# A conformer and sparse-attention trunk: one-column token sums and a GpSimd power in the norms, and a bias table skewed by 16 writes

## The chip, the cores and the metric

The kernel runs on one core of a Trainium2 chip. The metric is the device time of one execution in microseconds (us), as the median of three. The engines are TensorE (PE), VectorE (DVE), ScalarE (ACT) and GpSimd (POOL); SyncE (SP) here only issues DMA transfers. SBUF and PSUM are the two on-chip memories; PSUM has eight banks of 128x512 here.

## What is computed

Two layers of a decoder trunk on 512 tokens of width 1024 in float32. Layer 0 is a half-step SwiGLU feed-forward, a Conformer convolution module, a second feed-forward and a gated per-layer input embedding (ple); layer 1 has native sparse attention (nsa) in place of the convolution. Each part begins with an RMS norm, the convolution has a layer norm inside, and a last RMS norm ends the trunk. The parts that the change touches:

```python
def rms_norm(x, g):
    xf = x.astype(jnp.float32)
    y = xf * lax.rsqrt(jnp.mean(xf * xf, axis=-1, keepdims=True) + RMS_EPS)
    return (y * g.astype(jnp.float32)).astype(x.dtype)

def swiglu(x, wg, wu, wd):
    return (jax.nn.silu(x @ wg) * (x @ wu)) @ wd

def conformer_conv(h, w_pw1, b_pw1, w_dw, b_dw, ln_g, ln_b, w_pw2, b_pw2):
    u = h @ w_pw1 + b_pw1
    a, g = jnp.split(u, 2, axis=-1)
    u = a * jax.nn.sigmoid(g)
    u = lax.conv_general_dilated(...)  + b_dw      # depthwise, 31 taps, causal
    mu = jnp.mean(uf, axis=-1, keepdims=True)
    var = jnp.mean(jnp.square(uf - mu), axis=-1, keepdims=True)
    uf = (uf - mu) * lax.rsqrt(var + LN_EPS) * ln_g + ln_b
    return jax.nn.silu(uf) @ w_pw2 + b_pw2
```

Attention scores get a relative-position bias per head, rel_bias[bucket(t - s), head], for 16 heads.

## The kernel before

**Layout.** Activations lie transposed: tile k of x holds channels 128k to 128k+127 on the partitions and the 512 tokens along the free axis. So the sum over channels for a norm runs over partitions, and PE makes it by a product with a matrix of 1/1024.

**Weights.** They are streamed in units of 128x1024 (512 KB), in the order of their use. A float32 product is made of three passes, so each raw unit (`raw`, two buffers, loaded by SP at L201) is split: `wh` is the rounded copy (ACT, L219), `wl` the rest (L221, on POOL for the kinds in `CALM` from unit `CALM_FROM` on, else on DVE). Five buffers of each (`HLB`) run ahead of PE. L244 to L246 are the three passes, and a unit serves 24 matmuls. Inputs are split likewise: `prep` makes the high part on ACT (L292) and the low part on DVE (L293).

**Norms.** While a part adds its results to x, squares of the tiles are made and summed in `acc` (L309 to L313). `rfin` splits acc, `token_means` multiplies by the 1/1024 matrix (L344), which gives each token's mean on all partitions; `diagonal` reads out one value per token as a 128x4 tile (L336), `rsqrt` is a bit trick and three Newton steps on it (eleven DVE instructions, L322 to L327); `spread` transposes the result on PE back over all partitions (L353) and ACT copies it to R (L355). The first results of the next part are multiplied by R when they come out of PSUM. The order of PE puts the spreading some matmuls after the sums.

**Convolution.** The taps become block matrices for PE, made by POOL (L503). `tally` and `square` sum the filters' results and their squares about a mean `mid` taken from the first four tiles (`centre`). For the layer norm two products give the means (L693 and the line after it), `off` is the mean less mid (L697), `diagonal` reads both out, and eight times Y - off (POOL, L711), times R (DVE, L712), SiLU (ACT). PE works on `z_tiles`, p @ ple_w_in, as fill around it (`FILL`).

**The skewed table.** `bias_tables`, in the scheduler's order at the begin of ffn2 of layer 0, makes ext, a table of 16 heads x 640 distances on 16 partitions, and one DMA of the POOL queue writes it 128 times per head to DRAM, rows 641 apart (L745). In layer 1 `tt_load` reads it with rows 640 apart, so each key row comes shifted by one. `z_tiles` puts z into DRAM; it is read back in ple.

**The end.** `final` does the last norm in two halves of 256 tokens: sums, Newton, spreading (L1161), a copy Rf (L1163), and the scaling of eight tiles, five on DVE (L1172) and three on ACT and POOL (L1169, L1170).

**The order.** The code is issued once through; a scheduler of the language then decides each engine's order, and on an engine instructions run strictly in it. `high_priority(FIN_PRI)` moves instructions up.

Of the kernel before, what the change touches and what calls it, by code (L numbers as in the profile page):

```python
# [11 lines left out]
F32 = mybir.dt.float32  # L12
# [10 lines left out]
X_W1, SQ0, ADD0 = 4, 2, 4  # L23
# [4 lines left out]
CALM_FROM = 2  # L28
# [133 lines left out]
class Kern:  # L162
    def __init__(self, ctx, tc, aps):
# [31 lines left out]
    # -- weights --  # L195
    def _load(self, j):
        if KINDS[j] == "r":
            return
# [4 lines left out]

    def _split(self, j):
# [11 lines left out]
        if nsa and j % 4 in H_POOL:  # L216
            self.nc.gpsimd.tensor_copy(h[:, :w], t[:, :w])
        else:
            self.nc.scalar.activation(h[:, :w], t[:, :w], AF.Copy)  # L219
        eng = self.nc.gpsimd if calm or nsa and j % 4 in L_POOL else self.nc.vector  # L220
        eng.tensor_tensor(l[:, :w], t[:, :w], h[:, :w].bitcast(F32), op=OP.subtract)  # L221
        self.hl[j] = (h, l)

    def ahead(self, j):
        while self.next_split < min(j + 1, len(UNITS)):
            while self.next_raw < min(self.next_split + self.RAWB, len(UNITS)):
                self._load(self.next_raw)
# [3 lines left out]
        while self.next_raw < min(self.next_split + self.RAWB, len(UNITS)):  # L231
            self._load(self.next_raw)
# [15 lines left out]
    # -- small inputs --  # L248
# [25 lines left out]
    # -- norms: XH, XL = the two parts of x * g; R = 1 / rms along the free axis --  # L274
# [26 lines left out]
    def square_sum(self, k):  # L301
# [38 lines left out]
    def token_means(self, acc, eps):  # L340
# [946 lines left out]
```

## Time and profile before

| what | value |
|---|---|
| timed runs | 2169.51, 2168.81, 2167.43 us, median 2168.81 |
| profiled execution, span | 2167.5 us |
| PE busy | 2076.1 us (96%) |
| DVE busy | 1019.7 us (47%) |
| ACT busy | 830.8 us (38%) |
| POOL busy | 1051.4 us (49%) |
| DMA | 223.24 MB, mean 103 GB/s |

The page gives busy time by engine, groups of instructions by line, DMA issues with their landing, and the chain that ended last. The trace behind it gives timelines by engine, each with the idle time before an instruction and what ended it ("<-"). Durations of consecutive matmuls overlap, since they are pipelined; the distance between their starts is what one costs.

### The profile page before, as it was taken

How to read it: one execution, taken by the hardware profiler on the slowest of the kernel's cores; microseconds unless marked ns; L12 is line 12 of the kernel's file. 1: busy time of each engine (PE TensorE's matmuls, PEld its weight loads, DVE VectorE, ACT ScalarE, POOL GpSimd, SP SyncE). 2: the span in 40 equal slices, each digit the busy share in tenths (PEclk: the TensorE clock that was granted, in tenths of full speed). 3: DMA queues.
4: the chain of work that ended last, by engine and by line, in shares of the span. 5: the costliest groups of instructions: out<-in, count | busy, mean ns of one | idle time of the engine just before them, and what ended most of it. 6: DMA issues, size and time to landing. Idle time of an engine off the chain costs nothing. (4 is left out here: it accounts for less than half of the span.)

```text
span 2167.5 us, 25523 instructions
## 1 busy us (share of the span) xinstructions
PE 2076.1 (96%) x9546; PEld 1713.6 (79%) x9546; DVE 1019.7 (47%) x1889; ACT 830.8 (38%) x1393; POOL 1051.4 (49%) x653
## 2 busy tenths in 40 slices
PE   7999999899895999999999999999999999999997
PEld 6888888688674888888788888878888788888886
DVE  6430334797623312334743033355989673213336
ACT  4321234553522322234432123325888653223333
POOL 5444442784423444444444444556666444444441
PEclk9999999999997999999999999999999999999999
DMA  4222222244375222223322222454323032222222
GB/s 158 98 98 98 97 97 96 75 123 131 120 112 137 98 97 92 95 95 107 104 96 97 97 97 97 131 170 130 99 82 103 30 112 97 97 98 98 96 92 69
DMA packets 75882, 223.24 MB, mean 103 GB/s; under 512 B 8352, under 2 KB 16320, under 8 KB 75760
## 3 DMA queue, kind: packets, MB, share of 16 engines
q1 hardware_dynamic: 73728, 213.98, 29.6%
q0 software_dynamic: 1888, 7.59, 2.5%
q8 instruction: 75, 1.23, 0.2%
q14 instruction: 47, 0.39, 0.1%
q10 hardware_dynamic: 144, 0.07, 0.0%
HBM read 198.00 MB, written 16.25 MB: 99 GB/s over the span
## 5 line engine op out<-in xcount | busy, mean ns | idle before, releaser
L221 POOL TENSOR_TENSOR wl<-raw,wh 128x1024 fp32r<-128x1024 f32 (+1 forms) x315 | 787.6, 2502 | 900.6 <-ACT wh L219 871.5
L219 ACT ACTIVATE wh<-raw 128x1024 fp32r<-128x1024 f32 (+1 forms) x330 | 349.0, 1059 | 959.4 <-PE b L245 823.0
L244 PE MATMUL b<-s,wh 128*128 128x512 f32 x1728 | 678.8, 394 | 34.6 <-ACT R L355 22.8
L245 PE MATMUL b<-s,wh 128*128 128x512 f32 x1728 | 677.6, 392 | 6.1 <-DVE s L293 5.7
L246 PE MATMUL b<-s,wl 128*128 128x512 f32 x1728 | 677.2, 392 | 1.9 <-POOL wl L221 1.9
L244 PEld LDWEIGHTS b<-s,wh 128*128 128x128 f32 x1728 | 327.2, 189 | 103.7 <-ACT R L355 23.2
L245 PEld LDWEIGHTS b<-s,wh 128*128 128x128 f32 x1728 | 326.9, 189 | 77.2 <-DVE s L293 9.5
L246 PEld LDWEIGHTS b<-s,wl 128*128 128x128 f32 x1728 | 326.8, 189 | 71.2 <-POOL wl L221 2.8
L244 PE MATMUL b<-hid,wh 128*128 128x512 f32 x704 | 277.4, 394 | 0.0
L246 PE MATMUL b<-hid,wl 128*128 128x512 f32 x704 | 275.3, 392 | 0.0
L245 PE MATMUL b<-hid,wh 128*128 128x512 f32 x704 | 272.6, 388 | 0.0
L388 DVE TENSOR_TENSOR t<-b,R 128x512 f32<-128x512 f32 x88 | 60.8, 691 | 354.3 <-PE b L246 354.3
L426 DVE SCALAR_TENSOR_TENSOR s<-b,s 128x512 f32<-128x512 f32 x64 | 44.3, 692 | 331.2 <-PE b L246 331.2
L392 DVE TENSOR_TENSOR hid<-t,hid 128x512 fp32r<-128x512 f32 x88 | 170.2, 1937 | 53.4 <-ACT hid L391 53.2
L246 PEld LDWEIGHTS b<-hid,wl 128*128 128x128 f32 x704 | 132.2, 188 | 31.0
L245 PEld LDWEIGHTS b<-hid,wh 128*128 128x128 f32 x704 | 132.1, 188 | 29.6
L244 PEld LDWEIGHTS b<-hid,wh 128*128 128x128 f32 x704 | 132.3, 188 | 26.4
L386 DVE TENSOR_TENSOR t<-b,R 128x512 f32<-128x512 f32 x88 | 60.8, 691 | 166.5 <-PE b L246 96.0
L994 POOL TENSOR_SCALAR e<-e,sm,gates 128x512 f32<-128x512 f32 (+3 forms) x96 | 61.0, 640 | 41.2 <-DVE sm L988 35.6
L391 ACT ACTIVATE hid<-t 128x512 fp32r<-128x512 f32 x88 | 55.6, 633 | 55.9 <-DVE t L389 55.9
L389 DVE TENSOR_TENSOR t<-t,t 128x512 f32<-128x512 f32 x88 | 67.8, 774 | 8.0
L292 ACT ACTIVATE s<-s,small 128x512 fp32r<-128x512 f32 x48 | 38.0, 796 | 78.0 <-DVE s L426 34.9
(229 smaller groups left out, 2322.9 us busy)
## 6 DMA issues: line engine op xcount, KB each, us to landing
raw<-in_w SPq DMA_DIRECT2D x336, 512.0 KB, 3.5
skew<-tw POOLq DMA_DIRECT2D x1, 5120.0 KB, 56.4
z<-t SPq DMA_DIRECT2D x16, 256.0 KB, 2.4
z<-z SPq DMA_DIRECT2D x16, 256.0 KB, 3.3
tt<-skew SPq DMA_DIRECT2D x16, 256.0 KB, 2.8
wr<-in_w SPq DMA_DIRECT2D x8, 512.0 KB, 4.2
q<-t SPq DMA_DIRECT2D x32, 128.0 KB, 2.5
s<-in_xT SPq DMA_DIRECT2D x8, 256.0 KB, 6.1
```

The costliest lines, as they stand in the source:

```text
L219: self.nc.scalar.activation(h[:, :w], t[:, :w], AF.Copy)
L221: eng.tensor_tensor(l[:, :w], t[:, :w], h[:, :w].bitcast(F32), op=OP.subtract)
L244: mm(out, sh, mh, start=start, stop=False)
L245: mm(out, sh, ml, start=False, stop=False)
L246: mm(out, sl, mh, start=False, stop=stop)
L386: nc.vector.tensor_tensor(gr, pg, R, op=OP.mult)
L388: nc.vector.tensor_tensor(ur, pu, R, op=OP.mult)
L389: nc.vector.tensor_tensor(ur, ur, gr, op=OP.mult)
L391: nc.scalar.activation(h, ur, AF.Copy)
L392: nc.vector.tensor_tensor(l, ur, h.bitcast(F32), op=OP.subtract)
L426: nc.vector.scalar_tensor_tensor(self.xs[m], p, 0.5, self.xs[m], op0=OP.mult, op1=OP.add)
L994: nc.gpsimd.tensor_scalar(dst, dst, sm[:, a, bi:bi + 1], gate, op0=OP.mult, op1=OP.mult)
```

## The change

**Table.** ext goes to DRAM as `table`, 16x640. Each of 16 heads then has a DRAM tile of 128x641, written by one SP DMA that reads the head's table row 128 times (`skew_next`, called in `ffn` after each f above 2 while any is left). `tt_load` reads the tiles.

**Norms.** `rsqrt` is one POOL instruction, v to the power -0.5. `token_sums` makes one column per 128 tokens: the data tile is the stationary operand, one column of 1/1024 the moving one. `rfin(acc, True)`, for the two mix norms, takes the sums from acc at once, without the split and `diagonal`; the ffn and ple norms keep both. `spread_raw` leaves the result in PSUM.

**Layer norm.** off is made in its PSUM bank, the two sums come as columns (`mid0` is mid's column), the square of u is on ACT, Y - off moves from POOL to DVE, and Y times R reads R from PSUM.

**Final norm.** Its sums come as columns, and DVE's scalings read the spread values from PSUM.

**Start.** Unit 0 is loaded and split in halves, the order of the first loads is changed, 12 matmuls on constants run first, all squares are on ACT and all additions on DVE, and units 2 to 5 have their low parts on DVE (`CALM_FROM` 6).

```diff
-X_W1, SQ0, ADD0 = 4, 2, 4
+X_W1, WARM = 4, 12
...
-CALM_FROM = 2
+CALM_FROM = 6
...
+    def pieces(self, j, w):
+        return (slice(0, w // 2), slice(w // 2, w)) if j == 0 else (slice(0, w),)
...
+        self.power = self.cpool.tile([128, 4], F32, name="power")
+        nc.vector.memset(self.power, -0.5)
...
+        p = self.bank()
+        for n in range(WARM):
+            nc.tensor.matmul(p, self.meanr, self.meanr[:, None, :].to_broadcast([128, 4, 128]), start=True, stop=True)
...
         for k in range(KD):
-            if k in (0, X_W1):
-                self._load(self.next_raw)
-                self.next_raw += 1
+            if k in (0, 1, X_W1):
+                next(first[int(k == X_W1)])
...
-        start = (self.gname, self.gi) == ("ffn1_norm", 0)
-        if start and k < SQ0:
-            nc.gpsimd.tensor_tensor(sq, x, x, op=OP.mult)
-        else:
-            nc.scalar.activation(view(sq), x, AF.Square)
+        nc.scalar.activation(view(sq), x, AF.Square)
         if k:
-            (nc.gpsimd if start and k < ADD0 else nc.vector).tensor_tensor(self.acc, self.acc, sq, op=OP.add)
+            nc.vector.tensor_tensor(self.acc, self.acc, sq, op=OP.add)
...
-        nc.vector.tensor_scalar(i, v.bitcast(I32), 1, None, op0=OP.logical_shift_right)
-        nc.vector.tensor_scalar(y.bitcast(I32), i, -1, 0x5f3759df, op0=OP.mult, op1=OP.add)
-        for _ in range(3):
-            nc.vector.tensor_tensor(t, y, y, op=OP.mult)
-            nc.vector.scalar_tensor_tensor(t, t, -0.5, v, op0=OP.mult, op1=OP.mult)
-            nc.vector.scalar_tensor_tensor(y, t, 1.5, y, op0=OP.add, op1=OP.mult)
+    def rsqrt(self, v, n):
+        y = self.tiny.tile([128, 4], F32, name="r", tag="r")[:, :n]
+        self.nc.gpsimd.tensor_tensor(y, v, self.power[:, :n], op=OP.pow)
         return y
 
+    def token_sums(self, p, tiles):
+
+        for q in range(p.shape[1]):
+            for n, t in enumerate(tiles):
+                self.nc.tensor.matmul(p[:, q:q + 1], t[:, q * 128:q * 128 + 128], self.mean[:, :1],
+                                      start=n == 0, stop=n == len(tiles) - 1)
...
+                if soon:
+                    p = self.bank()[:, :4]
+                    self.token_sums(p, [acc])
+                    v = self.tiny.tile([128, 4], F32, name="v", tag="v")
+                    self.nc.vector.tensor_scalar(v, p, 1e-6, None, op0=OP.add)
+                    r = self.rsqrt(v, 4)
...
+                if f > 2:
+                    self.skew_next()
...
-        pm, pv = self.bank(), self.bank()
-        nc.tensor.matmul(pm, self.mean, self.total, start=True, stop=True)
-        nc.tensor.matmul(pv, self.mean, self.squares, start=True, stop=True)
-        for _ in range(FILL[1]):
+        off, pt = self.bank(), self.bank()
+        with self.tc.high_priority(FIN_PRI):
+            nc.tensor.matmul(off, self.mean, self.total, start=True, stop=True)
+            self.token_sums(pt[:, 0:4], [self.total])
+            self.token_sums(pt[:, 4:8], [self.squares])
+            u = self.tiny.tile([128, 4], F32, name="u", tag="u")
+            v = self.tiny.tile([128, 4], F32, name="v", tag="v")
+            nc.vector.tensor_tensor(u, pt[:, 0:4], self.mid0, op=OP.subtract)
+            nc.scalar.activation(u, u, AF.Square)
+            nc.vector.scalar_tensor_tensor(v, pt[:, 4:8], 1e-5, u, op0=OP.add, op1=OP.subtract)
+            r = self.rsqrt(v, 4)
+        nc.vector.tensor_tensor(off, off, self.mid, op=OP.subtract)
...
-            nc.gpsimd.tensor_tensor(Y[c], Y[c], off, op=OP.subtract)
+            nc.vector.tensor_tensor(Y[c], Y[c], off, op=OP.subtract)
             nc.vector.tensor_tensor(Y[c], Y[c], R, op=OP.mult)
...
-        self.skew = self.dpool.tile([16, 128 * 641], F32, name="skew")
-        nc.gpsimd.dma_start(self.skew.rearrange("h (p n) -> h p n", n=641)[:, :, :640],
-                            ext[:16, None, :].to_broadcast([16, 128, 640]))
+        self.table = self.dpool.tile([16, 640], F32, name="table")
+        nc.sync.dma_start(self.table, ext[:16, :])
+        self.skew = [self.dpool.tile([128, 641], F32, name=f"skew{h}") for h in range(16)]
+        self.unskewed = list(range(16))
+
+    def skew_next(self):
+
+        if self.unskewed:
+            h = self.unskewed.pop(0)
+            self.nc.sync.dma_start(self.skew[h][:, :640], self.table[h:h + 1, :].to_broadcast([128, 640]))
...
-                    nc.vector.scalar_tensor_tensor(o, x, self.col("final_norm", m), Rf, op0=OP.mult, op1=OP.mult)
+                    nc.vector.scalar_tensor_tensor(o, x, self.col("final_norm", m), p, op0=OP.mult, op1=OP.mult)
```

SP's queue at the begin of ffn2 of layer 0, `raw` being weight units and z tiles of the ple, before the change:

```order
L201 DMA raw_4108<-in_w 128x1024
L201 DMA raw_4120<-in_w 128x1024
L201 DMA raw_4132<-in_w 128x1024
L201 DMA raw_4271<-in_w 128x1024
L463 DMA z_6627<-z_72 128x512
L463 DMA z_6629<-z_72 128x512
L463 DMA z_6631<-z_72 128x512
L201 DMA raw_4298<-in_w 128x1024
```

The same place after it, where raw_4109 is unit 99 and raw_4264 unit 100:

```order
L207 DMA raw_4097<-in_w 128x1024
L775 DMA table<-tw_4225 16x640
L783 DMA skew_4234<-table 128x640
L783 DMA skew_4235<-table 128x640
L207 DMA raw_4109<-in_w 128x1024
L783 DMA skew_4236<-table 128x640
L783 DMA skew_4237<-table 128x640
L783 DMA skew_4238<-table 128x640
L207 DMA raw_4264<-in_w 128x1024
L783 DMA skew_4239<-table 128x640
L783 DMA skew_4240<-table 128x640
L783 DMA skew_4241<-table 128x640
```

Where before only weight loads and three z loads stood, the table and the 16 skew writes now stand between them; of those not shown five more come before the next raw (unit 101), then three, one z load, and unit 102.

POOL's queue at conv's mix norm, tw being taps, before the change:

```order
L503 TENSOR_TENSOR tw_2765<-bd,dw_2763 128x1152
L503 TENSOR_TENSOR tw_2767<-bd,dw_2763 128x1152
L503 TENSOR_TENSOR tw_2769<-bd,dw_2763 128x1152
L503 TENSOR_TENSOR tw_2771<-bd,dw_2763 128x1152
L554 TENSOR_TENSOR y_2707<-y_2707,t_2709 128x512
```

The same place after it, `power` being a constant tile of -0.5:

```order
L528 TENSOR_TENSOR tw_2754<-bd,dw_2750 128x1152
L528 TENSOR_TENSOR tw_2756<-bd,dw_2750 128x1152
L528 TENSOR_TENSOR tw_2758<-bd,dw_2750 128x1152
L331 TENSOR_TENSOR r<-v,power 128x4
L579 TENSOR_TENSOR y_2694<-y_2694,t_2696 128x512
L579 TENSOR_TENSOR y_2694<-y_2694,t_2699 128x512
```

The power that makes r follows the last of the eight taps; before, POOL had no part in the norm, whose steps were on DVE.

DVE's queue at the layer norm, from off (L697) to the diagonal reads of v, before the change:

```order
L697 TENSOR_TENSOR sum_3736<-b_3732,sum_3535 128x512
L336 ISA junk,v<-b_3733,ident 128x128
L336 ISA v 128x1
L336 ISA junk,v<-b_3733,ident 128x128
L336 ISA v 128x1
```

Further on before the change, from the last read of u to the first Newton step:

```order
L336 ISA u 128x1
L699 TENSOR_TENSOR u<-u 128x4
L700 SCALAR_TENSOR_TENSOR v<-v,u 128x4
L322 TENSOR_SCALAR ir<-v 128x4
L323 TENSOR_SCALAR yr<-ir 128x4
L325 TENSOR_TENSOR tr<-yr 128x4
L326 SCALAR_TENSOR_TENSOR tr<-tr,v 128x4
```

The same place after it, b_3726 being off's bank and b_3791 that of the spread r:

```order
L731 TENSOR_TENSOR b_3726<-b_3726,sum_3522 128x512
L741 TENSOR_TENSOR y_2694<-y_2694,b_3726 128x512
L741 TENSOR_TENSOR y_2749<-y_2749,b_3726 128x512
L741 TENSOR_TENSOR y_2860<-y_2860,b_3726 128x512
L741 TENSOR_TENSOR y_2971<-y_2971,b_3726 128x512
L741 TENSOR_TENSOR y_3082<-y_3082,b_3726 128x512
L741 TENSOR_TENSOR y_3241<-y_3241,b_3726 128x512
L741 TENSOR_TENSOR y_3393<-y_3393,b_3726 128x512
L741 TENSOR_TENSOR y_3517<-y_3517,b_3726 128x512
L727 TENSOR_TENSOR u<-b_3727,m_3529 128x4
L729 SCALAR_TENSOR_TENSOR v<-b_3727,u 128x4
L742 TENSOR_TENSOR y_2694<-y_2694,b_3791 128x512
```

The eight subtractions of off stand on DVE now, ahead of u and v; before they were on POOL, and DVE went from off to the diagonal reads.

## Rows read from the trace of the kernel before

**Rows 1.** PE's waits, by line and what ended them: total, times, longest us

```profile
PE b L244 <- ACT R L355: 22.8, 1, 22.8
PE b L353 <- DVE yr L327: 18.4, 3, 9.2
```

**Rows 2.** Windows from 609 to 690 us: busy (instructions) by engine, PEclk, DMA, GB/s

```profile
609.20:640.00 30.80, 28.46 (x127) 23.32 (x126) 7.57 (x24) 5.30 (x7) 7.39 (x4) 1.00 0.95 142
640.00:655.50 15.50, 13.35 (x48) 9.95 (x48) 0.00 (x0) 1.17 (x2) 4.73 (x2) 0.89 1.02 147
655.50:678.20 22.70, 0.00 (x0) 0.00 (x0) 0.00 (x1) 3.65 (x4) 5.09 (x3) 0.60 0.72 156
678.20:690.00 11.80, 11.78 (x40) 9.50 (x41) 11.59 (x15) 7.06 (x10) 6.72 (x3) 0.77 0.28 93
```

**Rows 3.** ACT's timeline: start, duration us, instruction, idle before and what ended it

```profile
540.34 1.06 ACT L219 ACTIVATE wh<-raw 128x1024 fp32r<-128x1024 f32 x1 [0.57 <-PE b L245]
...
610.49 0.57 ACT L741 ACTIVATE tw<-b 16x512 f32<-16x512 f32 x1
...
639.06 1.06 ACT L219 ACTIVATE wh<-raw 128x1024 fp32r<-128x1024 f32 x1 [23.12 <-DMA raw<-in_w]
...
669.50 1.06 ACT L219 ACTIVATE wh<-raw 128x1024 fp32r<-128x1024 f32 x1 [21.85 <-DMA raw<-in_w]
...
677.59 0.58 ACT L355 ACTIVATE R<-b 128x512 f32<-128x512 f32 x1
```

**Rows 4.** DMA from 605 to 690 us: queues (packets, MB, share), issues (landing us)

```profile
q0 software_dynamic: 1058, 5.26, 56.1%
q1 hardware_dynamic: 1872, 6.03, 19.6%
...
skew<-tw POOLq DMA_DIRECT2D x1, 5120.0 KB, 56.4
```

**Rows 5.** DMA issues of the whole run: KB each, median us to landing

```profile
z<-t SPq DMA_DIRECT2D x16, 256.0 KB, 2.4
```

**Rows 6.** PE's timeline at the start, conv's mix norm, layer norm, final norm

```profile
7.02 0.79 PE L244 MATMUL b<-s,wh 128*128 128x512 f32 x1 [7.02 <-ACT s L292]
...
30.51 0.39 PE L344 MATMUL b<-t,meanr 128*128 128x512 f32 x1
...
405.10 1.11 PE L353 MATMUL b<-ident,yr 128*128 128x128 f32 x4 [9.24 <-DVE yr L327]
...
551.62 1.08 PE L353 MATMUL b<-ident,yr 128*128 128x128 f32 x4 [8.28 <-DVE yr L327]
552.36 0.78 PE L244 MATMUL b<-zp,wh 128*128 128x512 f32 x1
...
2158.55 0.69 PE L1161 MATMUL b<-ident,yr 128*128 128x128 f32 x2 [5.26 <-DVE yr L327]
```

**Rows 7.** DVE's timeline at the same four places

```profile
22.71 0.74 DVE L293 SCALAR_TENSOR_TENSOR s<-s,small,s 128x512 fp32r<-128x512 f32 x1
...
391.39 2.05 DVE L322 TENSOR_SCALAR ir<-v 128x4 int32<-128x4 int32 x1
...
541.27 1.26 DVE L336 CUSTOM_DVE_ANT_0 junk<-sum,ident 128x128 f32<-128x128 f32 x1
...
2159.70 3.56 DVE L1172 SCALAR_TENSOR_TENSOR hid<-s,small,hid 128x256 f32<-128x256 f32 x5 [1.20 <-ACT hid L1163]
```

**Rows 8.** POOL's timeline at conv's mix norm and at the layer norm

```profile
385.03 18.82 POOL L503 TENSOR_TENSOR tw<-bd,dw 128x1152 f32<-128x1152 f32 x8 [9.96 <-DMA dw<-in_dw]
...
537.23 10.16 POOL L711 TENSOR_TENSOR y<-y,sum 128x512 f32<-128x512 f32 x8 [1.23 <-DVE sum L697]
```

**Rows 9.** Groups of instructions: count, busy us, mean ns, idle before

```profile
L221 POOL TENSOR_TENSOR wl<-raw,wh 128x1024 fp32r<-128x1024 f32 (+1 forms) x315 | 787.6, 2502 | 900.6 <-ACT wh L219 871.5
...
L388 DVE TENSOR_TENSOR t<-b,R 128x512 f32<-128x512 f32 x88 | 60.8, 691 | 354.3 <-PE b L246 354.3
...
L994 POOL TENSOR_SCALAR ec<-ec,sm,gates 128x7 f32<-128x7 f32 x16 | 6.4, 400 | 5.4 <-DVE sm L988 3.3 <-ACT s L972 1.3 <-PE b L1014 0.8
```

More of the change, by code (lines that the diff above doesn't have):

```diff
@@ L174, in __init__ @@
         self.raw, self.hl = {}, {}
+        self.unskewed = []
         self.RAWB, self.HLB = 2, 5
@@ L215, in _split @@
         nsa, calm = what.startswith("nsa"), j >= CALM_FROM and what.startswith(CALM)
-        if nsa and j % 4 in H_POOL:
-            self.nc.gpsimd.tensor_copy(h[:, :w], t[:, :w])
-        else:
-            self.nc.scalar.activation(h[:, :w], t[:, :w], AF.Copy)
         eng = self.nc.gpsimd if calm or nsa and j % 4 in L_POOL else self.nc.vector
-        eng.tensor_tensor(l[:, :w], t[:, :w], h[:, :w].bitcast(F32), op=OP.subtract)
+        for c in self.pieces(j, w):
+            if nsa and j % 4 in H_POOL:
+                self.nc.gpsimd.tensor_copy(h[:, c], t[:, c])
+            else:
+                self.nc.scalar.activation(h[:, c], t[:, c], AF.Copy)
+            eng.tensor_tensor(l[:, c], t[:, c], h[:, c].bitcast(F32), op=OP.subtract)
         self.hl[j] = (h, l)
@@ L231, in ahead @@
         while self.next_raw < min(self.next_split + self.RAWB, len(UNITS)):
[L232 removed]
+            drain(self._load(self.next_raw))
             self.next_raw += 1
@@ L346, in token_means, with spread_raw @@
         nc.vector.tensor_scalar(v, v, eps, None, op0=OP.add)
-        return v
+        return self.rsqrt(v, 4)
+    def spread_raw(self, r, n=4):
+        p = self.bank()[:, :n * 128]
+        for q in range(n):
+            self.nc.tensor.transpose(p[:, q * 128:q * 128 + 128], r[:, q:q + 1].to_broadcast([128, 128]), self.ident)
+        return p
     def spread(self, r):
         nc = self.nc
-        p = self.bank()
-        for q in range(4):
-            nc.tensor.transpose(p[:, q * 128:q * 128 + 128], r[:, q:q + 1].to_broadcast([128, 128]), self.ident)
+        p = self.spread_raw(r)
         R = self.cpool.tile([128, 512], F32, name="R", tag="R", bufs=1)
@@ L581, in centre @@
         nc.scalar.activation(self.mid, p, AF.Copy, scale=KD / EARLY)
+        p = self.bank()[:, :4]
+        self.token_sums(p, [self.total])
+        self.mid0 = self.tiny.tile([128, 4], F32, name="m0", tag="m0")
+        nc.vector.tensor_scalar(self.mid0, p, KD / EARLY, None, op0=OP.mult)
         for c, y in self.done:
@@ L690, in conv @@
             next(fill)
-        pm, pv = self.bank(), self.bank()
-        nc.tensor.matmul(pm, self.mean, self.total, start=True, stop=True)
-        nc.tensor.matmul(pv, self.mean, self.squares, start=True, stop=True)
-        for _ in range(FILL[1]):
-            next(fill)
-        off = self.ptile("sum", 4)
-        nc.vector.tensor_tensor(off, pm, self.mid, op=OP.subtract)
-        v, u = self.diagonal(pv, "v"), self.diagonal(off, "u")
-        nc.vector.tensor_tensor(u, u, u, op=OP.mult)
-        nc.vector.scalar_tensor_tensor(v, v, 1e-5, u, op0=OP.add, op1=OP.subtract)
-        r = self.rsqrt(v, 4, "r")
-        for _ in range(FILL[2]):
-            next(fill)
-        R = self.spread(r)
+        off, pt = self.bank(), self.bank()
[10 more added lines that the diff above has]
+        nc.vector.tensor_tensor(off, off, self.mid, op=OP.subtract)
+        for _ in range(FILL[1] + FILL[2]):
+            next(fill)
+        R = self.spread_raw(r)
         for _ in fill:
@@ L751, in tt_load @@
             h = g * HPG + a
-            self.nc.sync.dma_start(t, self.skew[h, 127:127 + 128 * 640].rearrange("(p n) -> p n", n=640)[:, :512])
+            flat = self.skew[h].rearrange("p n -> (p n)")
+            self.nc.sync.dma_start(t, flat[127:127 + 128 * 640].rearrange("(p n) -> p n", n=640)[:, :512])
             self.TT[g, a] = t
@@ L851, in cmp_in @@
         if first:
-            fin = self.rfin(self.acc)
+            fin = self.rfin(self.acc, True)
         for gp in range(2):
@@ L1150, in norm @@
         def norm(hs, squares):
-            p = self.bank()[:, :256]
-            nc.tensor.matmul(p, self.mean, acc[:, hs], start=True, stop=False)
-            for n, t in enumerate(squares):
-                nc.tensor.matmul(p, self.mean, t, start=False, stop=n == LATE - 1)
-            v = self.diagonal(p, "v", 2)
-            nc.vector.tensor_scalar(v, v, 1e-6, None, op0=OP.add)
-            r = self.rsqrt(v, 2, "r")
+            p = self.bank()[:, :2]
+            self.token_sums(p, [acc[:, hs]] + squares)
+            v = self.tiny.tile([128, 4], F32, name="v", tag="v")[:, :2]
+            nc.vector.tensor_scalar(v, p, 1e-6, None, op0=OP.add)
+            r = self.rsqrt(v, 2)
             yield
-            p = self.bank()[:, :256]
-            for q in range(2):
-                nc.tensor.transpose(p[:, q * 128:q * 128 + 128], r[:, q:q + 1].to_broadcast([128, 128]), self.ident)
+            p = self.spread_raw(r, 2)
             Rf = self.ptile("hid", 24)[:, :256]
```

33 lines of the change are left out of this document (17 added, 16 removed).

## Prediction

> **What bounds the kernel now.** I read the page's busy times first, then the list of PE's waits, the windows of the stage that it names, and there the timelines and the queues. TensorE (PE) works 2076.1 of 2167.5 us (table above), so only the 91 us in which it stands idle, and what it then does at the lower clock, can be won. The waits say where: 22.8 us at once for ACT's R, and 18.4 us before the spreading transposes at L353 for DVE's yr [rows 1]. The windows put the first into its stage. Between 609.2 and 690 us, ffn2 of layer 0, PE is idle 2.3 us at the end of the first window, 2.15 in the second, all of the third (22.7): 27.2 us [rows 2]. The same rows show the granted clock at 0.89, 0.60 and 0.77. The first window has 127 matmuls in 28.46 us, 0.224 each; at that pitch the 48 and 40 of the second and fourth would take 10.8 and 9.0 us, and they took 13.35 and 11.78. Records can be missing, so I count 4 of these 5.4 us as clock. That hole costs about **31 us**.
>
> Why it is there: ACT's weight copies waited for raw 23.12 and 21.85 us, and the R copy that PE wanted came behind them, at 677.59 [rows 3]. Meanwhile the queues show one transfer of 5120 KB with 56.4 us to landing. Its 5.26 MB held 56.1% of the 16 engines over 85 us, 47.7 us or 110 GB/s, where the weight queue beside it moved 6.03 MB in 19.6%, 16.7 us or 361 GB/s [rows 4].
>
> **Part 1, the skewed table.** It goes from one POOL-queue write out of 16 SBUF partitions to one small write of the table and 16 SP writes of 320 KB, DRAM to DRAM. In SP's order (above) they are not spread over the feed-forward: two stand ahead of raw 99, five ahead of raw 100, 13 ahead of raw 101, 16 ahead of raw 102. So every byte now stands ahead of weights. Let one write take T. The table can start when ACT's tw copy ends, 611.1 [rows 3], and lands 2.4 us later, as a z tile does [rows 5]: 613.5. Raw 102 then lands at 613.5 + 16 T + 4 loads of 1.5 us (512 KB at 361 GB/s) + 2.4 of latency = 621.9 + 16 T. PE wanted unit 99 at 637.7 (its first stall ends at 640.2 after 2.5) and takes 24 x 0.229 = 5.5 us a unit, so unit 102 is due at 654.2, and its raw 3.5 us before (copy 1.06 [rows 3], subtraction 2.5 [rows 9]): 650.7. The stall is 16 T - 28.8, or nothing for T below 1.8 us.
> No row shows a DRAM-to-DRAM write. Bounds: 0.9 us at the weight queue's 361 GB/s, 3.5 us at before's 56.4 / 16 [rows 4]. Ordinary transfers between DRAM and 128 partitions, 256 KB in 2.4 us with all latency [rows 5], are nearest, since the 16 source partitions are what sets before's transfer apart; writes queue one behind another, so I take T = 1.8 and a residue of 1 us: **-30** (0 to -31). The POOL queue loses one issue of 1 us, which costs nothing.
> On this the row is the 110 GB/s beside 361 in one window. The Trainium skill, "SBUF — State Buffer", section "Door 1: The DMA port swizzle", says that a transfer's rate follows from how many of 16 ports its partitions reach; partitions 0 to 15 reach four, an estimate of 109 GB/s, which the trace's 110 agrees with, and by it the new source is free of that limit. "DMA: Bandwidth & Descriptors", section "Issuing engines are not separate DMA queues", speaks against the change: all queues end on the same 16 engines, so another issuer saves nothing by itself; that is rival A.
>
> **Part 2, the start.** PE's first matmul is at 7.02 and its first L344 (58th in its order) at 30.51 [rows 6]: 23.5 us for 57 matmuls that need 13, while ACT and DVE make x0 to x7's parts. The change gives the start's squares to ACT, the additions to DVE, and the low parts of units 2 to 5 to DVE, so POOL does nothing there. ACT's order is now half unit 0, a square, half, a square, then x0: first matmul at about 8.0 instead of 7.0 (two squares of 0.6 more, as R's copy of the same width takes [rows 3], minus the half copy). DVE then has eight low parts of 0.74 [rows 7], seven additions of that width at 0.7 and three weight subtractions of twice the width at 1.5: 15 us from about 7.5, so the 58th instruction comes at 23 to 24. **-6** (-4 to -8). Twelve warm-up matmuls run in idle time; if the clock has fallen again by 8 us, the start is as slow as before's first matmuls, inside that range.
>
> **Part 3, conv's mix norm.** PE waits 9.24 us until 405.10 [rows 6]. Small DVE steps on 128x4 took some 2.05 us each while POOL made its eight taps (385.03 for 18.82 us) [rows 7, 8]. The eleven Newton steps become one POOL power; but by POOL's order (above) it stands behind all eight taps. Without DVE beside them the taps may go at 2.1 to 2.3 us instead of 2.35, so they end at 402 to 403.5; then the power. Nearest rows for it: POOL on 128x7, 0.40 us [rows 9], and no row for a power at all: 0.4 to 3 us, taken as 0.6. The spread then starts at 403: **-2** (-3 to +1). The sums come earlier than before, which gains nothing behind that queue.
>
> **Part 4, layer norm.** PE waits 8.28 us until 551.62 [rows 6]. Four diagonal reads of u, from SBUF, took up to 1.26 us each beside POOL's eight subtractions (537.23 for 10.16) [rows 7, 8]. Now the sums come as columns and there is no diagonal; but all eight Y - off are on DVE, ahead of u and v in its order (above). From 537.2, where POOL's began, they take 8 x 0.69 = 5.5 us (a DVE operation of that width with a PSUM operand, a mean over 88 with POOL mostly busy beside them [rows 9]), then u, ACT's square and v to 543.5. The power waits on POOL behind one weight subtraction of 2.5 us, whose copy ends at 541.4 [rows 3, 9]: to 543.9, so r at 544.5. PE, with its extra passes, is there at about 544. Stall 0 to 1 instead of 8.28, and the low clock after it goes (the first matmul after it, at 552.36, takes 0.78 us [rows 6]; some 11 at the lower level, 0.2 us longer each: 2.2): **-9** (-5 to -10.5). The copy of R goes too, off the path; R and off hold two PSUM banks longer, which I cost at nothing while z's fill needs one at a time, and at 1 us if not.
>
> **Part 5, the rest.** NSA's mix norm is what remains of L353's 18.4 us, 0.9: **-1**. The ffn and ple norms: PE has work over their Newton steps already, and the power stands behind at most one 2.5 us subtraction: 0. The final norm: r is waited for until 2158.55 [rows 6], after five scalings on DVE, and the last work is five more, 3.56 us beside POOL [rows 7]. Now these read PSUM (about 0.4 each, half the width of the 0.69 [rows 9]) and no copy stands ahead of them: 1.6 us at each of two places, less a power behind nothing: **-3** (-2 to -4). Extra one-column passes: centre 8, mix norms 8 each, layer norm 16, less one full-width product, at 0.13 to 0.19 us (four transposes from 551.62 took 0.74 [rows 6]): **+2** (1 to 4).
>
> **Sum.** -30 - 6 - 2 - 9 - 1 - 3 + 2 = -49. The profiled span is 2167.5, 1.3 under the median of 2168.8; I take the difference as constant: 2118.5 + 1.3 = **2120**.
>
> **Rivals.** A: the bytes, not their source, hold the weights up. T stays near 3.5, the stall is 16 x 3.5 - 28.8 = 27 us with its clock, and only the other 19 us are won: **2150**; at T = 2.5 it is 11 + 2, so 2132. For it: same bytes, same 2564-byte row pitch, same engines, now ahead of weights in one queue. Against: the weight queue's 361 GB/s beside it.
> B, on the other side: 128 rows read the same 2560 bytes of DRAM over and over. If that one place serves the reads in turn, T is above that of before. The point is where the stall and its 4 us eat 31 + 19 us: 16 T - 28.8 = 46, T = 4.7 us, 70 GB/s. At T = 6 the stall is 67: 2168.8 - 50 + 71 = **2190**. For it: no row shows such reads. Against: the tt loads read that DRAM region at 256 KB in a few us.
> C: the powers don't pay. At 3 us each, mix norm, layer norm and both halves of the end lose 2.4 each, 9.6 in all: **2130**.
>
> **How the numbers follow.** Forecast (T under 2.2) 0.70, 2107 to 2127; A 0.17, 2128 to 2166; C 0.06; B 0.07. The low end takes every term at its best (31 + 8 + 3 + 10.5 + 1 + 4 - 1 = 56.5, 2112) and 5 us for stalls of a us or two in nsa that move. The high end takes in A at 3.5 us: 2107 to 2152; what is left out is B and A's tail, 0.15 with the low side. A measurement of this kernel tells 0.2% (4 us) from no change: faster 0.88, same 0.04 (A near T = 4.5), slower 0.08.
>
> **What would show it.** Right: the 16 skew writes land within about 30 us of 614, no ACT wait for raw above 5 us between 610 and 680, granted clock near 1 there; PE's wait at the layer norm under 2 us, at conv's mix norm still about 7, with POOL's taps as what ended last before the power; the first L344 at 23 to 24 us; POOL's power under 1 us. Wrong: a raw wait that ends with a skew write's landing (A or B, by T), power rows of 2 us and more (C), or PE waiting for a PSUM bank behind off and R.

## The result, and the profile after

The changed kernel takes 2117.24 us (median of 4; 2116.84 to 2119.84) against 2169.16 us of the kernel before beside it: a ratio of 0.9767, 95% interval 0.9753 to 0.9781. The prediction was 2120 us, 2107 to 2152. The profiled execution's span is 2115.1 us, 52.4 under before's 2167.5; PE is busy 2067.5 us of it (98%).

The first two lines of PE's list of waits after the change (us in total, times, longest):

```profile
PE b L363 <- POOL r L331: 12.2, 3, 9.6
PE b L636 <- DMA uu<-ud: 7.2, 2, 3.9
```

Two lines of the same list before, beside those of [rows 1]:

```profile
PE b L1161 <- DVE yr L327: 6.8, 2, 5.3
PE b L607 <- DMA uu<-ud: 3.1, 1, 3.1
```

The 22.8 us for R [rows 1] are gone. All spreads are on L363 now, the final norm's too: they wait 12.2 us for POOL's power, where those of before waited for DVE's yr 18.4 us [rows 1] and, in the final norm (L1161), 6.8. The wait for uu, the convolution's input from DRAM, has grown from 3.1 to 7.2. The windows of [rows 2], the same times:

```profile
609.20:640.00 30.80, 30.80 (x139) 25.49 (x138) 4.57 (x15) 6.78 (x8) 10.88 (x6) 1.00 0.92 263
640.00:655.50 15.50, 15.50 (x70) 12.81 (x70) 13.51 (x12) 7.83 (x11) 10.06 (x5) 1.00 0.42 134
655.50:678.20 22.70, 22.70 (x102) 18.80 (x101) 11.14 (x12) 8.24 (x10) 12.60 (x6) 1.00 0.44 140
```

PE is busy throughout at a granted clock of 1.00, and the DMA engines move 263 GB/s in the first window where they moved 142. ACT's timeline there, to hold against [rows 3], and the DMA issues (KB, median us to landing) against [rows 4]:

```profile
613.71 1.06 ACT L230 ACTIVATE wh<-raw 128x1024 fp32r<-128x1024 f32 x1 [7.28 <-DMA raw<-in_w]
619.01 1.06 ACT L230 ACTIVATE wh<-raw 128x1024 fp32r<-128x1024 f32 x1 [4.24 <-DMA raw<-in_w]
630.65 1.06 ACT L230 ACTIVATE wh<-raw 128x1024 fp32r<-128x1024 f32 x1 [10.58 <-DMA raw<-in_w]
```

```profile
skew<-table SPq DMA_DIRECT2D x16, 320.0 KB, 9.6
```

Weights still queue behind the writes, up to 10.58 us, but PE has no idle time in these windows: the buffers ahead of it cover the wait. Thirteen writes and three units lie between the first write's issue, 604.94 in SP's timeline, and 630.65. With the prediction's load time and latency an estimate of one write is (25.7 - 3 x 1.5 - 2.4) / 13 = 1.45 us.

PE's timeline at the places of [rows 6], and at conv's first filter (448.92):

```profile
24.63 0.40 PE L355 MATMUL b<-t,meanr 128*128 128x512 f32 x1
...
398.68 1.12 PE L363 MATMUL b<-ident,r 128*128 128x128 f32 x4 [9.57 <-POOL r L331]
...
448.92 10.95 PE L636 MATMUL b<-uu,tw 128*128 128x128 f32 x72 [3.90 <-DMA uu<-ud]
...
544.53 0.65 PE L363 MATMUL b<-ident,r 128*128 128x128 f32 x4 [1.57 <-POOL r L331]
...
2107.45 0.69 PE L363 MATMUL b<-ident,r 128*128 128x128 f32 x2 [1.10 <-POOL r L331]
```

POOL's timeline at conv's mix norm and the layer norm, as [rows 8]:

```profile
377.97 19.66 POOL L528 TENSOR_TENSOR tw<-bd,dw 128x1152 f32<-128x1152 f32 x8 [9.96 <-DMA dw<-in_dw]
397.59 1.04 POOL L331 TENSOR_TENSOR r<-v,power 128x4 f32<-128x4 f32 x1
...
541.11 2.40 POOL L231 TENSOR_TENSOR wl<-raw,wh 128x1024 fp32r<-128x1024 f32 x1 [5.33 <-ACT wh L230]
543.45 1.03 POOL L331 TENSOR_TENSOR r<-v,power 128x4 f32<-128x4 f32 x1
```

DVE's at the same two and at the end, as [rows 7]:

```profile
380.64 0.16 DVE L387 TENSOR_SCALAR v<-b 128x4 f32<-128x4 f32 x1 [4.93 <-PE b L338]
...
536.96 4.87 DVE L741 TENSOR_TENSOR y<-y,b 128x512 f32<-128x512 f32 x8
...
2108.60 2.05 DVE L1206 SCALAR_TENSOR_TENSOR hid<-s,small,b 128x256 f32<-128x256 f32 x5 [1.98 <-ACT hid L1197]
```

At the convolution's norm v is ready at 380.8, and its power waits 17 us behind the taps. At the layer norm the power follows one weight subtraction, as the prediction had it.

**Where the 52 us come from.** The same product (counted by the first passes, L244 and L254) stands in both timelines. The table gives, stretch by stretch, how its lead changes in these two executions; minus is earlier after the change:

| stretch | predicted us | measured us |
|---|---|---|
| start | -6 | -5.9 |
| rest of ffn1, layer 0 | | -1.3 |
| conv's mix norm | -2 | +0.3 |
| conv's filters on PE | | +6.8 |
| layer norm | -9 | -9.7 |
| ffn2's hole (table) | -30 | -32.5 |
| ple, ffn1 of layer 1 | | -2.7 |
| nsa's mix norm | -1 | -1.3 |
| rest of nsa | | -2.3 |
| ffn2, ple of layer 1 | | -1.1 |
| end | -3 | -2.8 |
| extra passes | +2 | in the rows above |
| sum | -49 | -52.5 |

Single rows vary between executions of the same code. In the runs whose start is the changed kernel's, the first product of the norm's sums comes between 24.2 and 25.8 us. In a_skew_dram, whose edit lies behind them, conv's filters come out at +5.0 and the layer norm at -7.4.

### The profile page after: what moved, and what is told of

Read it like the earlier page. It is cut to its first block, busy times and chain, and to the rows that moved or that the text cites. A ratio compares the mean times of both kernels' runs of the same rounds, so it can differ in the third digit from the quotient of the medians.

```text
span 2115.1 us, 25526 instructions
## 1 busy us (share of the span) xinstructions
PE 2067.5 (98%) x9608; PEld 1715.7 (81%) x9608; DVE 966.9 (46%) x1744; ACT 830.1 (39%) x1394; POOL 1030.9 (49%) x646
## 3 DMA queue, kind: packets, MB, share of 16 engines
q1 hardware_dynamic: 76208, 219.26, 32.5%
## 5 line engine op out<-in xcount | busy, mean ns | idle before, releaser
L231 POOL TENSOR_TENSOR wl<-raw,wh 128x1024 fp32r<-128x1024 f32 x311 | 778.1, 2503 | 866.4 <-ACT wh L230 862.3
L254 PE MATMUL b<-s,wh 128*128 128x512 f32 x1728 | 676.0, 392 | 4.8 <-ACT s L308 3.5
L255 PE MATMUL b<-s,wh 128*128 128x512 f32 x1728 | 674.6, 390 | 1.9 <-DVE s L309 1.6
L254 PEld LDWEIGHTS b<-s,wh 128*128 128x128 f32 x1728 | 325.4, 188 | 74.5 <-ACT s L308 5.7
L255 PEld LDWEIGHTS b<-s,wh 128*128 128x128 f32 x1728 | 325.3, 188 | 70.1 <-DVE s L309 3.0
L254 PE MATMUL b<-hid,wh 128*128 128x512 f32 x704 | 273.9, 389 | 0.0
L255 PE MATMUL b<-hid,wh 128*128 128x512 f32 x704 | 273.2, 389 | 0.0
L254 PEld LDWEIGHTS b<-hid,wh 128*128 128x128 f32 x704 | 132.1, 188 | 27.6
L255 PEld LDWEIGHTS b<-hid,wh 128*128 128x128 f32 x704 | 132.1, 188 | 27.4
```

The source lines that it names most:

```text
L231: eng.tensor_tensor(l[:, c], t[:, c], h[:, c].bitcast(F32), op=OP.subtract)
L254: mm(out, sh, mh, start=start, stop=False)
L255: mm(out, sh, ml, start=False, stop=False)
```

## The experiments

Four theories were open: what held the table's transfer (its source, its queue or its size); what each norm's place holds; what conv's filters lost; and why products far from any edit run faster. "After" below is the changed kernel. All but a_skew_sbuf were timed in rounds against the kernel before.

| run | us | against before (interval) |
|---|---|---|
| a_skew_pool | 2158.39 | 0.9961 (0.9948 to 0.9974) |
| a_skew_dram | 2118.18 | 0.9771 (0.9758 to 0.9784) |
| a_skew_sbuf | 2287.0 | one run |
| a_r_first | 2105.04 | 0.9707 (0.9694 to 0.972) |
| a_ln_pool | 2124.82 | 0.98 (0.9788 to 0.9813) |
| a_start_old | 2123.31 | 0.9792 (0.9777 to 0.9807) |
| a_warm0 | 2118.31 | 0.977 (0.9757 to 0.9783) |
| a_final_R | 2120.06 | 0.9777 (0.9764 to 0.979) |
| b_pad32 | 2168.48 | 1.0004 (0.9995 to 1.0012) |
| b_pad64 | 2174.63 | 1.0034 (1.0021 to 1.0047) |
| b_pad192 | 2160.85 | 0.9969 (0.9958 to 0.9981) |
| a_pad32 | 2131.97 | 0.9834 (0.9821 to 0.9846) |

**The table as before, a_skew_pool.**

```diff
-        nc.sync.dma_start(self.table, ext[:16, :])
...
+        nc.gpsimd.dma_start(self.skew.rearrange("h (p n) -> h p n", n=641)[:, :, :640],
+                            ext[:16, None, :].to_broadcast([16, 128, 640]))
```

> The changed kernel with only the skewed table as before: one POOL-queue transfer of 5120 KB out of 16 SBUF partitions. Theory (the term -30 of the prediction): the hole in ffn2 of layer 0 comes back whole, ACT's waits for raw of 20 us and more, the transfer lands after some 56 us, PE idle 25 to 29 us between 600 and 670, 2147 to 2151 us. Rival (the hole had other causes, such as POOL's and DVE's slower norms, that the change took away as well): less than half of it, under 2132.

Measured 41 us over after, more than the 30 to 34 expected and more than the whole hole. Lines of its ACT, PE and DVE timelines and the issue's landing say why:

```profile
629.19 1.06 ACT L230 ACTIVATE wh<-raw 128x1024 fp32r<-128x1024 f32 x1 [23.41 <-DMA raw<-in_w]
...
659.31 0.80 PE L355 MATMUL b<-t,meanr 128*128 128x512 f32 x1 [39.40 <-DVE t L379]
...
658.56 0.69 DVE L379 TENSOR_TENSOR t<-acc,t 128x512 fp32r<-128x512 f32 x1 [57.11 <-DMA skew<-tw]
```

```profile
skew<-tw POOLq DMA_DIRECT2D x1, 5120.0 KB, 57.6
```

ACT waits for weights again, as before. But PE's wait ends with the norm's t, and t waited for the transfer itself: in this program's layout that buffer (from byte 136128 to 138176) overlaps ext, which the transfer reads (from 137888). Before it did not (ext at 152256). So the rival falls, but the hole that came back is not quite that of before, where PE waited for R behind the weights. By the same product this stretch is 41.1 us longer than in after, and before's 32.5. That the 8.6 between them are the overlap is read from these rows; no run moves the buffer alone. The changed kernel, which frees ext after the small write, has neither.

**One transfer, from DRAM, a_skew_dram,** the same queue and size as before:

```diff
         nc.sync.dma_start(self.table, ext[:16, :])
-        self.skew = [self.dpool.tile([128, 641], F32, name=f"skew{h}") for h in range(16)]
...
+        self.skew = self.dpool.tile([16, 128 * 641], F32, name="skew")
+        nc.gpsimd.dma_start(self.skew.rearrange("h (p n) -> h p n", n=641)[:, :, :640],
+                            self.table[:, None, :].to_broadcast([16, 128, 640]))
```

> The changed kernel with the small table in DRAM, but then one single POOL-queue transfer of 5120 KB from DRAM to DRAM. It tells the source from the queue and from the cutting into 16. Source theory (16 partitions held the transfer to 110 GB/s): it lands in 15 to 30 us, weights come late by at most a few us, PE has no wait over 3 us there, 2115 to 2121 us. Rival 1 (one big transfer on another queue shares the 16 engines packet by packet and starves the weights whatever its source): landing over 45 us and 2140 or more. Rival 2 (rows 2564 bytes apart are slow to write): the same, 2140 or more.

Measured 2118.18, the time of after; the landing, 31.2 us, is just above the 15 to 30 expected. Its DMA view from 590 to 680 us (queue: packets, MB, share of 16 engines):

```profile
q0 software_dynamic: 1072, 5.32, 22.7%
...
skew<-table POOLq DMA_DIRECT2D x1, 5120.0 KB, 31.2
```

5.32 MB in 22.7% of 90 us, 20.4 us, are 260 GB/s where [rows 4] give 110. The source theory holds: queue, size and row pitch of the target are those of before, and the cutting into 16 makes no difference to the time.

**Sixteen SP writes, each from one partition of SBUF, a_skew_sbuf:**

```diff
-        self.table = self.dpool.tile([16, 640], F32, name="table")
-        nc.sync.dma_start(self.table, ext[:16, :])
...
+        for h in range(16):
+            nc.sync.dma_start(self.skew[h][:, :640], ext[h:h + 1, None, :].to_broadcast([1, 128, 640]))
```

> The changed kernel with 16 SP writes, each of one head's row, out of SBUF (one partition each) and not out of DRAM. Source theory: all 16 rows lie on the same 16 partitions as before the change, so together they need the 48 to 56 us that the one transfer needed, now in the queue ahead of weights: a hole of 15 to 40 us, 2132 to 2160 us. Rival (pieces in SP's queue are what helped): 2115 to 2121 us.

Far slower than either expected, 170 us over after. Two of its windows (as in [rows 2]) and a line of DVE's timeline:

```profile
610.00:650.00 40.00, 9.25 (x41) 7.32 (x39) 0.00 (x0) 0.00 (x0) 1.29 (x1) 0.67 0.91 27
...
700.00:760.00 60.00, 0.00 (x0) 0.00 (x0) 0.00 (x0) 0.00 (x0) 0.00 (x0) 0.50 0.89 30
```

```profile
786.29 0.69 DVE L379 TENSOR_TENSOR t<-acc,t 128x512 fp32r<-128x512 f32 x1 [180.94 <-DMA skew<-tw]
```

The DMA engines are 90% busy and move 27 GB/s: 320 KB in about 12 us, as if one partition were read at a time; that the 16 rows would together reach the 110 GB/s was wrong. Here too t waits for the writes that read ext, so the run's time is not the weights' wait alone; the rate is what it tells. With 110 from 16 partitions and 260 from DRAM this settles the source. It agrees with the Trainium skill, "SBUF — State Buffer", section "Door 1: The DMA port swizzle", by which the rate follows from how many of 16 ports, 435 GB/s together, the partitions reach: an estimate from it is 27 for one port and 109 for four.

**The power ahead of the taps, a_r_first.** The taps read a copy of bd that depends on r, so POOL's order turns around:

```diff
...
                 next(fin)
+                bd = self.phase.tile([128, CG], F32, name="bd2")
+                nc.gpsimd.tensor_scalar(bd, self.bd, self.r_mix[:, :1], 0.0, op0=OP.mult, op1=OP.is_gt)
+                self.bd = bd
```

> The changed kernel with the power of conv's mix norm ahead of POOL's eight taps: the taps read a copy of bd that POOL makes from r. It tells what the queue on POOL holds at this norm. v is there at 380.8 us and PE gets to the spread at 389.1, so r is at 382 and the taps end some 4 us later than now, at 402, while PE first needs them at 445. Theory: PE's wait of 9.6 us and the low clock after it (2 us) go, and DVE's conv work starts 9 us earlier, 2105 to 2108 us. Rival (PE then waits as much longer for uu, since DVE's work between R and the write of ud sets the time of the first filter on PE): 2112 to 2117 us.

Measured 2105.04, 12 us under after and the fastest of all. Its POOL and PE timelines:

```profile
381.82 1.04 POOL L331 TENSOR_TENSOR r<-v,power 128x4 f32<-128x4 f32 x1 [12.89 <-DVE v L387]
382.97 0.41 POOL L686 TENSOR_SCALAR bd<-bd,r 128x32 f32<-128x32 f32 x1
383.45 20.39 POOL L528 TENSOR_TENSOR tw<-bd,dw 128x1152 f32<-128x1152 f32 x8
```

```profile
389.87 0.60 PE L363 MATMUL b<-ident,r 128*128 128x128 f32 x4
...
436.53 8.28 PE L636 MATMUL b<-uu,tw 128*128 128x128 f32 x72 [2.49 <-DMA uu<-ud]
```

No wait before the spread. The first filter on PE waits 2.49 instead of 3.90 us and runs 72 products in 8.28 instead of 10.95: the rival, that uu would take the gain back, falls. By the same product its lead over after is 11.0 us behind the spread and 12.5 at the end.

**Y - off back on POOL, a_ln_pool.**

```diff
...
-            nc.vector.tensor_tensor(Y[c], Y[c], off, op=OP.subtract)
+            nc.gpsimd.tensor_tensor(Y[c], Y[c], off, op=OP.subtract)
```

> The changed kernel with the eight subtractions Y - off back on POOL, as before, and off in SBUF for it; the column sums and the power stay. By POOL's order the power then stands behind all eight. Theory (as the prediction costs this norm): POOL is busy with them from 537.2 to 547, so r comes at 548 to 549 and PE waits 5 to 6 us instead of 1.6, with 2 us of low clock: 2121 to 2125 us. Rival (the column sums alone made the gain): 2116 to 2119 us.

7.6 us over after. By the same product 5.9 us are lost at this place, where PE waits 4.82 us for the power; the profiled execution also has 0.9 us more at the start, which the edit does not touch, 0.8 more up to the sums and 0.9 more in nsa. POOL's timeline:

```profile
538.46 9.93 POOL L742 TENSOR_TENSOR y<-y,sum 128x512 f32<-128x512 f32 x8 [1.23 <-DVE sum L732]
548.36 1.01 POOL L331 TENSOR_TENSOR r<-v,power 128x4 f32<-128x4 f32 x1
```

The power comes 4.9 us later than after's 543.45. So column sums and power alone give some 4 of the 9.7 us; the larger part is that POOL is free for the power.

**The old start, a_start_old, and no warm-up, a_warm0.**

```diff
-X_W1, WARM = 4, 12
+X_W1, SQ0, ADD0, WARM = 4, 2, 4, 0
...
-CALM_FROM = 6
+CALM_FROM = 2
...
```

> The changed kernel with the start of before: unit 0 in one piece, the old order of the loads, no warm-up matmuls, two squares and three additions on POOL, the low parts of units 2 to 5 on POOL. Theory (the term -6 of the prediction): the first L355 at 30 to 31 us instead of 24.6, and the lag stays to the end, 2121 to 2125 us. Rival (the lag is swallowed by the waits of conv, where PE waits for uu 3.9 us anyway): 2117 to 2119 us.

6.1 us over after: the term stands, and the lag is not swallowed (by the same product it is 4.0 us in ffn1 and 5.3 behind conv's filters). (This edit also takes back the halves, the loads' order and the engines of squares and sums.) The first product of the sums is at 28.66, not at 30 to 31: 1.9 us of the lead at the start lie in none of these edits, and no run shows where.

```diff
-X_W1, WARM = 4, 12
+X_W1, WARM = 4, 0
```

> The changed kernel without the 12 warm-up matmuls alone. In the changed kernel the first five products from 8.46 us stand at the high clock, those from 11.06 to 13.8 at the low one (0.43 us apart). Theory 1: the warm-up gives the high clock to the first few and nothing else; without it the low clock lasts until 14 to 15 us and the first L355 comes at 24.6 to 26, 2117 to 2119 us. Theory 2 (the low clock would last several us longer): 27 us or later and 2119 to 2122 us.

2118.31, no difference clear of noise; the first L355 is at 23.37, since eight products fewer stand ahead of it in PE's order, while the same product comes 0.6 us later than in after. The last two products at the wide pitch without the warm-up:

```profile
14.53 0.59 PE L255 MATMUL b<-s,wh 128*128 128x512 f32 x1
14.95 0.40 PE L256 MATMUL b<-s,wl 128*128 128x512 f32 x1
```

The same with it, in after, and after's window ahead of it (as in [rows 2]):

```profile
13.79 0.57 PE L254 MATMUL b<-s,wh 128*128 128x512 f32 x1
14.20 0.39 PE L255 MATMUL b<-s,wh 128*128 128x512 f32 x1
...
11.00:13.80 2.80, 2.74 (x7) 2.16 (x8) 2.80 (x5) 2.80 (x7) 0.00 (x0) 0.50 0.81 288
```

Either way products stand some 0.42 us apart until 14.2 or 15.0 us, and 0.23 from there on. After the warm-up PE idles from 6.8 to 8.5 and then works with gaps, and from 11.0 to 13.8 us the granted clock is 0.50, the lower of its two levels (1.2 of 2.4 GHz). Without the warm-up the profile lists 1.00 for this stretch; that it was the lower level too is read from the pitch alone.

**R from SBUF in the final norm, a_final_R.**

```diff
-                    nc.vector.scalar_tensor_tensor(o, x, self.col("final_norm", m), p, op0=OP.mult, op1=OP.mult)
+                    nc.vector.scalar_tensor_tensor(o, x, self.col("final_norm", m), Rf, op0=OP.mult, op1=OP.mult)
```

> The changed kernel with DVE's scalings of the final norm reading the copied R from SBUF and not the bank, as before. Theory (half of the term -3 of the prediction): five scalings beside POOL take 3.5 us instead of 2.05 at both places, 2118.5 to 2121 us by the end, the last scaling 1.5 us and the second spread up to 1.5 us later. Rival (the first five lie beside PE's work): 1.5 us in all, 2117.5 to 2119.5 us.

2.8 us over after by the medians. The intervals against before overlap, so the size rests on the trace: from the last products with px to the end the run has 2.7 us more. DVE's lines, to hold against after's 2.05 above and 2.04 below them:

```profile
2100.45 3.56 DVE L1206 SCALAR_TENSOR_TENSOR hid<-s,small,hid 128x256 f32<-128x256 f32 x5 [0.21 <-ACT hid L1197]
...
2109.85 3.56 DVE L1206 SCALAR_TENSOR_TENSOR hid<-s,small,hid 128x256 f32<-128x256 f32 x5 [1.97 <-ACT hid L1197]
```

The first five in after:

```profile
2100.68 2.04 DVE L1206 SCALAR_TENSOR_TENSOR hid<-s,small,b 128x256 f32<-128x256 f32 x5 [0.21 <-ACT hid L1197]
```

Both fives are 1.5 us longer and both count; reading the bank is the whole gain at the end, 2.8 in the table.

**Places in SBUF: b_pad32, b_pad64, a_pad32, b_pad192.** The table's rows without a term are mostly ffn, with no edit in them. There hid's products are closer together after the change: the first down product of ffn1 has 288 and goes from 149.10 to 214.81 before, from 143.25 to 208.30 after, 65.7 and 65.05 us. Page lines of before (count, busy us, mean ns):

```profile
L244 PE MATMUL b<-hid,wh 128*128 128x512 f32 x704 | 277.4, 394 | 0.0
L246 PE MATMUL b<-hid,wl 128*128 128x512 f32 x704 | 275.3, 392 | 0.0
```

And of after:

```profile
L254 PE MATMUL b<-hid,wh 128*128 128x512 f32 x704 | 273.9, 389 | 0.0
L256 PE MATMUL b<-hid,wl 128*128 128x512 f32 x704 | 273.2, 389 | 0.0
```

The second pass, L245 and L255, has 388 and 389 ns: what changed are the two passes around it.

The four kernels add unused bytes per partition, the first ahead of the weights, the others (`tiny.tile([128, 16])` for 64, 8 columns for 32, 48 for 192) behind them and ahead of hid.

```diff
+        self.pad = self.cpool.tile([128, 4], F32, name="pad")
+        nc.vector.memset(self.pad, 0.0)
```

> The kernel before with one unused constant tile of 16 bytes a partition, which moves every tile behind it by 32 bytes. In the profile of the changed kernel the products with hid and px as moving operand stand 0.2266 us apart and before it 0.2289 and 0.2292, over 2112 and 310 of them: 5 us that no term of the prediction holds. Layout theory (hid and px lie at an odd multiple of 32 bytes before, at a multiple of 64 after): pitch 0.2266 for hid, 2163 to 2165 us. Rival (the pitch follows other engines' work or is one execution's): 0.229, 2167 to 2171 us.

No change; the form "hid's own place" falls.

```diff
+        self.pad = self.tiny.tile([128, 16], F32, name="pad", tag="pad", bufs=1)
+        tc.nc.vector.memset(self.pad, 0.0)
```

> The kernel before with one unused tile of 64 bytes a partition behind the weights and the slots of x, ahead of everything of a phase. The 32 bytes ahead of the weights left hid's pitch at 0.2290, so what counts cannot be hid's place alone. Layout theory, second form: what counts is the distance of the moving tile from the weight tile that is loaded meanwhile, modulo 128 bytes: x's parts at 0 stand 0.2270 us apart in every run, hid and px at 64 before and with 32 bytes 0.2290 and 0.2292, at 0 in the changed kernel 0.2266 and 0.2272, tw and zp at 32 or 96 0.2332 to 0.2342. With 64 bytes hid and px come to 0: pitch 0.2266, 5 us less, 2162 to 2164 us. Rival (something else of the change): 0.2290 and 2167 to 2170 us.

> The changed kernel with 32 unused bytes at the same place, which puts hid and px at 32 and tw and zp at 0 modulo 128 from the weights. Layout theory, second form: hid and px as slow as tw and zp were, 0.232 to 0.2335, and tw and zp at 0.2266: 2112 x 0.0062 + 310 x 0.006 - 280 x 0.0065 = 13 us more, 2128 to 2132 us. Rival: 2116 to 2119 us.

The first came out the other way, 6.5 us slower where 5 faster was expected; the second as expected, 15 us slower. Modulo 128 falls with the first; modulo 256 sorts both, and was put to the test with 192 bytes.

> The kernel before with 192 unused bytes a partition at the place of the 64. Those put hid's pitch at 0.2333 and not at 0.2266, so modulo 128 is refuted. Taken modulo 256, the distance of the moving tile from the weight tiles sorts all pitches seen: 0 gives 0.2266 to 0.2272 (x's parts everywhere, hid and px after the change, tw with 32 bytes there), 64 gives 0.2290 (before, and with 32 bytes ahead of the weights), 32, 96, 128, 160 and 224 give 0.231 to 0.234. 192 bytes bring hid and px of the kernel before to 0. Layout theory, third form: hid at 0.2266, px at 0.227, 5.6 us less than before, 2161 to 2164 us. Rival (the pitch is not set by this distance): 0.229 or 0.233, 2167 us or more.

7.6 us faster than before, where 5.6 was expected; the 2 us more were not taken apart. Mean distance of hid's 2112 products, and the place of hid less that of the weight tiles modulo 256, from the built programs:

| kernel | place | us apart |
|---|---|---|
| before, b_pad32 | 64 | 0.2290, 0.2290 |
| b_pad64 | 128 | 0.2333 |
| b_pad192 | 0 | 0.2267 |
| after | 0 | 0.2267 |
| a_pad32 | 32 | 0.2333 |

Another tile bears it out: in a_pad32 tw, the layer norm's result, comes from 224 to 0, and its products go from 0.2333 to 0.2268 us apart. hid's products take 476.9 us together after and 481.7 before. So 4.8 us of the change's 52, and 0.5 for px's products of full width, are the 16 bytes of `power` and the smaller norm tiles, which happened to move hid by -64 against the weights.

## Why the prediction was right

- **The table.** Mechanism and size held: the rate from 16 partitions, T = 1.45 us where 1.8 was taken, no stall, 32.5 us for 30. One of its signs did not come: weights waited up to 10.58 us where none above 5 was expected, and the buffers covered it. The clock's share was set too low: 32.5 less the 27.2 idle leaves 5.3; the windows gave 5.4, and the sum cut it to 4. Rivals A and B fall with a_skew_dram: the same bytes and pitch, another source.
- **The start** gave 5.9 for 6, of which a_start_old takes back 4.0; the first product of the sums is at 24.63, where 23 to 24 was expected. The warm-up, costed within the range, gives nothing.
- **Conv's mix norm** is the step that failed. "Without DVE beside them the taps may go at 2.1 to 2.3 us": they took 19.66 us for eight, 2.46 each, against 18.82 [rows 8] with DVE's steps among them, and the power 1.04 for 0.6. So nothing was won: PE waited 9.57 us for 9.24, where about 7 was expected. The order was read rightly, and a_r_first shows what it costs: 12 us.
- **Conv's filters** were not in the sum. DVE's and ACT's work between R and the write of ud stands ahead of the first filter's input. R, the write of ud and the first filter before:

```profile
406.25 0.60 ACT L355 ACTIVATE R<-b 128x512 f32<-128x512 f32 x1 [6.97 <-PE b L353]
446.45 0.33 SPq L520 DMA_DIRECT2D ud<-t  x1
451.77 8.20 PE L607 MATMUL b<-uu,tw 128*128 128x128 f32 x72
```

R and ud after, and the first window of the filter (as in [rows 2]):

```profile
399.84 0.60 ACT L370 ACTIVATE R<-b 128x512 f32<-128x512 f32 x1 [9.81 <-PE b L363]
443.88 0.33 SPq L545 DMA_DIRECT2D ud<-t  x1
...
448.90:452.00 3.10, 3.08 (x14) 3.08 (x15) 3.10 (x6) 1.70 (x2) 0.00 (x0) 0.50 0.18 73
```

R and ud in a_r_first:

```profile
391.24 0.58 ACT L370 ACTIVATE R<-b 128x512 f32<-128x512 f32 x1
431.00 0.33 SPq L545 DMA_DIRECT2D ud<-t  x1
```

From R to ud it took 44.0 us after, 40.2 before and 39.8 in a_r_first. PE came 6.9 us earlier than before, waited 3.90 and began the first filter at the lower granted clock, 0.50 (10.95 for 8.20): 6.65 of the 6.8 us. So a lead may be lost in a stretch that other engines pace, but it need not be: a_r_first kept its own. Why the stretch was 3.8 us longer in the changed kernel no run shows.

- **Layer norm** came as worked out: subtractions 4.87 for 5.5, spread at 544.53 for 544.5 (what was won ahead of it was lost again in conv's filters, so the two clocks compare), wait 1.57 for 0 to 1.
- **The end** held, 2.8 for 3, and a_final_R gives all of it to the reads of the bank.
- **Extra passes** were priced too high in the sum: eight columns start at 379.66 and the next product at 380.47, 0.10 us each for 0.13 to 0.19. **The power** at 0.70 (128x2) to 1.04 us (128x4) is above the 0.6 taken and far from rival C's 3.
- **Not foreseen at all:** hid's and px's place, -5.3. It was luck that this and the table's surplus of 2.5 make up for most of conv's two misses (+6.8, +2.3), so the total is closer than its terms.

The other 2.3 us in nsa were not taken apart by a run.

## What to carry to other kernels

Before blaming a queue for a slow transfer, work out its own rate from its share and bytes, and ask how many partitions it reads from: a broadcast out of 16 partitions held up weights at 110 GB/s, and the same through DRAM left PE without a wait there. An operation moved to a fast engine is as late as what stands ahead of it in that engine's order, so move the queue, not only the operation. Compare the pitch of products that no edit touched: a few bytes of layout were worth 5 us here.

## What the runs showed of the hardware

In these six kernels the pitch of a 128x512 product goes with the place of its moving tile against the weight tiles in SBUF modulo 256 bytes: for hid it is 0.2267 us at 0, 0.2290 at 64, and 0.2333 at 32 and 128. Weight loads run beside the products (25.49 of 30.80 us in the window from 609.2); why the distance matters no run shows. A transfer from one SBUF partition moved 27 GB/s (a_skew_sbuf), from 16 neighbouring ones 110 (before), from DRAM to DRAM 260 (a_skew_dram). A power on POOL took 1.03 us on 128x4 and 0.70 on 128x2 (after). DVE's scaling of 128x256 from PSUM beside POOL took 0.41 us (after), from SBUF 0.71 (a_final_R).
